# Short convolutions in PSUM and inverse roots by a power on GpSimd, in a hybrid attention and experts block

## The chip, the cores and the metric

The kernel runs on one core of a Trainium2 chip. A core has five engines with instruction queues of their own, each worked off in order: PE (matrix products), DVE (VectorE), ACT (ScalarE), POOL (GpSimd) and SP, which here only issues transfers. PE writes to PSUM, which has eight banks of 2 KB per partition; DVE and ACT read and write PSUM and SBUF, POOL only SBUF in this kernel. The metric is the device time of one execution in microseconds, as the median of three runs.

## The reference

One block over 256 latent tokens and 256 context tokens, 2048 features, all in float32. Cut to what bears on the change:

```python
h  = modulate(rms_norm(x, norm1_g), ...);  hc = modulate(rms_norm(ctx, norm1_g), ...)
glu, qkv, z, ab, br = split_in_proj(h @ w_in)          # and of hc
qkv = silu(dw_conv(qkv, short_w))                      # 5 taps along the tokens, per feature
q = q * rsqrt(sum(q*q, -1) + EPS) * 128 ** -0.5        # per head of 128 features
k = k * rsqrt(sum(k*k, -1) + EPS)
# per head, in both directions: gated delta rule in chunks, context first, then latents
o = rms_norm(o, dn_norm_g) * silu(z)
y = (sigmoid(br_a) * conv_module(glu) + sigmoid(br_b) * (o @ w_dn_out)) @ w_out
x = x + m2 * y
x = x + m5 * peer_experts(modulate(rms_norm(x, norm2_g), ...))
return rms_norm(x, final_g)
```

The convolution module has a layer norm of its own. So the inverse square root of a sum occurs in the norm of the inputs, of each head's q and k, of each head's output o, in the layer norm, in norm2 and in the final norm.

## The kernel before

**The weight stream.** All weights come from HBM as half tiles of 128 x 1024 float32. `prep` turns a half tile into two parts whose sum is exact: ACT casts `whi` (L201) and POOL or DVE subtracts `wlo` (L205); the table `SPLIT` says which, and for the heads ("a") it is always POOL. `mm3` (L209 to L212) makes one *product* of a block of 128 x 128 weights and 128 x 256 activations from three matmuls, `hi*hi + hi*lo + lo*hi`. `products` runs a weight tile's products into a PSUM bank `ps_p` per sequence, from a pool `psg` of three banks; the other five banks belong to the work between.

**The order.** All instructions of an engine stand in an order that is fixed when the kernel is built. Other work is written as generators, *chains*: a chain yields the number of products that are to be issued before its next step, by the table `GAP`. Several chains are under way at once, so steps of one head lie between steps of another on each engine's queue.

**The heads.** Sixteen heads follow each other. A head has 96 products (v 32, k 32 over both sequences, q 16 and z 16 over the latents alone), each projection followed by `short_conv` (z by a gate):

```python
for s in range(n):
    nc.scalar.copy(pd[:, s, 2:T + 2], ps[s])                                              # L593
    nc.scalar.activation(dst[:, s, :], ps[s], AF.Copy, scale=swh[:, blk, 2:3])            # L594
...
for i in (0, 1, 3, 4):
    nc.vector.scalar_tensor_tensor(dst, pd[:, :n, i:i + T], swh[:, blk, i:i + 1], dst, ALU.mult, ALU.add)  # L597
```

then a tanh on ACT (L600) and a last multiply on DVE (L602). `pd` is one of two padded buffers in SBUF, `dst` the result in SBUF. After q, the chain of a head goes through `prepare` (norms, keys and values by tokens, decays), `invert` (the triangular inverse, blocks doubling) and `scan` (four chunks, both directions). In `prepare`, sums of squares by ACT (L656, L666) get EPS on DVE (L667), their inverse root by `newton_steps` (L323, then three times L326, L328, L330, all on DVE, on 128 x 6 elements, with a gap of three products after each of the ten steps), and then, per direction, PE makes a decay's exponent (`ps_D`, L700 to L702), ACT its exponential (L704), DVE L709, L710 and L713, ACT L715, DVE L717 and POOL L718. The next direction's `ps_D` needs L713. In `scan`, the output's sums (L902) go through L904, `newton_steps` on 128 x 2 and a product with the factor of q (L907) to the scaling of `oacc` (L910), which PE transposes (L914).

**Elsewhere.** `inverse_rms` (L334) makes the same steps for the inputs, the layer norm, norm2 (L1269) and the final norm (L1522); the last two run with nothing beside them (`whole`).

After the heads come the first convolution gates, the branches' projections, `w_out` with norm2, the routing of the experts, their two dense passes, and the final norm.

Of the kernel before, what the change touches and what calls it, by code (L numbers as in the profile page):

```python
# [23 lines left out]
P = 128  # L24
D = 2048
# [21 lines left out]
GAP = dict(N=3, C0=3, C=3.5, P0=0.5, Pv=3, Pk=4, Pq=3, Pn=2.5, PG=3, PA=3.5, PD=2.5, Pat=2, Pkh=2, Pkl=1, L0=4,  # L47
           LX=4, LY=4.5, F0=7, FX=5, FY=5, FZ=2, IT=4.5, E=4, Z1=5, Z2=7, Sv=4, Sr=4, Sn=5, SS=6, So=3.5,
           Ss=1, Sf=3, Sa=2, Sg=5, So2=3,
           M=10, M0=2, DC=12, M1=16, MT=3, V=1.75, VA=2, VS=4.5, LN=4, NW=1, W=7, D=24, RT=5, RC=7, RB=11, H0=21, HP=12, G0=4)  # L50

# columns of the constants
# [5 lines left out]
# the parts of the modulation vectors in their order: vector, first column, columns  # L58
# [6 lines left out]
# columns of the parameters  # L65
# [35 lines left out]
# bytes per partition, buffers  # L101
# [27 lines left out]
def body(ctx: ExitStack, tc: tile.TileContext, a: dict, out: bass.AP):  # L129
# [14 lines left out]
    # A raw float32 half tile becomes two float32r parts whose sum is exact.  # L144
# [69 lines left out]
    # A chain is a generator: it yields how many products to issue before its next step.  # L214
# [22 lines left out]
    def products(keys, acts, sink, first):  # L237
        """The products of weight tiles, side by side, with each of the activations; what follows each."""
        pss = [[cur["psg"].tile([P, T], F32, name="ps_p", tag="g") for _ in acts] for _ in keys]
        halves = 1 if keys[0][0] == "peer_v" else 2  # L240
        for u in range(halves):
            ws = [parts.pop(0) for _ in keys]
            assert [w[0] for w in ws] == keys, (ws, keys)
            for c in range(8):
                for ps, (_, wh, wl) in zip(pss, ws):
                    for p_, (ah, al) in zip(ps, acts):
                        mm3(p_, wh[:, c, :], wl[:, c, :], ah[u][:, c, :], al[u][:, c, :],
                            u == 0 and c == 0, u == halves - 1 and c == 7)
# [28 lines left out]
    def mod_stream(mods, depth):  # L277
        """The weights' tiles for the parts mods of the vectors, loaded ahead of their products."""
# [14 lines left out]
    def mod_part(v, at, w, sc, alloc, psum_tile, following, gap):  # L293
        """Columns at ... at + w of vector v, one weight tile per step."""
# [12 lines left out]
        # column at + g * n + j * 128 + i at row 32 g  # L307
# [12 lines left out]
    def newton_steps(x, shape, gap, tag="sm"):  # L320
        """1 / sqrt(x) by Newton's steps from an estimate by the exponent."""
        y, t = cur["work"](shape, tag=tag, name="rsy"), cur["work"](shape, tag=tag, name="rst")
        nc.vector.tensor_scalar(y.bitcast(I32), x.bitcast(I32), -0.5, 1597463007.0, ALU.mult, ALU.add)  # L323
        yield gap
        for _ in range(3):
            nc.vector.tensor_tensor(t, y, y, ALU.mult)  # L326
            yield gap
            nc.vector.scalar_tensor_tensor(t, t, -0.5, x, ALU.mult, ALU.mult)  # L328
            yield gap
            nc.vector.scalar_tensor_tensor(y, t, 1.5, y, ALU.add, ALU.mult)  # L330
            yield gap
        return y

    def inverse_rms(acc, tag="d"):  # L334
        """1 / the root of the features' mean square, on every partition, from its sums per partition."""
# [8 lines left out]
        y = yield from newton_steps(ms, [P, n], GAP['NW'])  # L344
# [9 lines left out]
    if True:  # L354
# [63 lines left out]
        def scales(q):  # L418
            """For the feature chunks of part q."""
# [72 lines left out]
        # -30000 where a decay is of the future or of the token itself  # L492
# [23 lines left out]
        def decays():  # L516
# [8 lines left out]
            # column: chunk, direction, (a | b), head  # L525
# [22 lines left out]
            # log1p(e) = ln(u) + (e - (u - 1)) / u  # L548
# [15 lines left out]
            # sums of g from the chunk's first token, after the token, over the chunk  # L564
# [18 lines left out]
        def short_conv(ps, blk, dst):  # L583
            n = len(ps)
# [7 lines left out]
            for s in range(n):  # L592
                nc.scalar.copy(pd[:, s, 2:T + 2], ps[s])  # L593
                nc.scalar.activation(dst[:, s, :], ps[s], AF.Copy, scale=swh[:, blk, 2:3])  # L594
            yield GAP['C0']
            for i in (0, 1, 3, 4):
                nc.vector.scalar_tensor_tensor(dst, pd[:, :n, i:i + T], swh[:, blk, i:i + 1], dst, ALU.mult, ALU.add)  # L597
                yield GAP['C'] * n / 2
            th = pd[:, :n, 2:T + 2]
            nc.scalar.activation(th, dst, AF.Tanh)  # L600
            yield GAP['C'] * n / 2
            nc.vector.scalar_tensor_tensor(dst, th, 1.0, dst, ALU.add, ALU.mult)  # L602
# [29 lines left out]
        def prepare(x):  # L632
            """Norms, the keys and values by tokens, the products of keys, all decays."""
# [33 lines left out]
            nc.vector.tensor_scalar(ss, ss, EPS, None, ALU.add)  # L667
            yield GAP['Pq']
            rs = yield from newton_steps(ss, [P, 6], GAP['N'])
            rk = rs[:, 0:4]  # L670
            x.rq = work([P, 2], tag="sm")
            nc.vector.tensor_scalar(x.rq, rs[:, 4:6], float(P) ** -0.5, None, ALU.mult)
# [22 lines left out]
            # decay[j, i] = exp(sum of g over j < m <= i), then K = decay * (k_j . k_i)  # L695
# [26 lines left out]
        def invert(x):  # L722
            """The inverse of I + diag(beta) K^T per chunk and direction: blocks double in half
            precision, then two terms of the residual's series."""
# [50 lines left out]
            def product(lhs, rhs, name):  # L775
                """Per direction: a bank with the products of the four chunks."""
# [21 lines left out]
            # E = I - A T, then Z (I + E + E E)^T  # L798
# [26 lines left out]
        def scan(x):  # L825
            """The chunks in their order, both directions side by side; o, normed and gated."""
# [18 lines left out]
            for n in range(4):  # L845
# [36 lines left out]
                if n >= 2:  # L882
# [4 lines left out]
                    # each chunk of o is reached first by one direction, then by the other  # L887
# [38 lines left out]
        def glu_a(n, ps):  # L926
# [6 lines left out]
            nc.scalar.activation(half_a[n], ps[0], AF.Copy, scale=0.5)  # L933
            yield 1

        def glu_b(n, ps):
            ut = cur["work"]([P, T], tag="ut")
            nc.scalar.activation(ut, ps[0], AF.Tanh, scale=0.5)
# [9 lines left out]
        def taps(n, pr, cw, dst, gap):  # L948
            """The convolution over a raster row of chunk n of the features."""
# [14 lines left out]
        def convolution_a():  # L964
            """The first chunks, beside the last head's scan; they wait in DRAM for the others."""
# [16 lines left out]
        def follow(x, ps):  # L982
            """After a head's last projection."""
# [19 lines left out]
        first_jobs = [(("w_in", 64), (0, 1)), (("w_in", 48), (0, 1)), (("w_in", 32), (1,))]  # L1003
        free = [psg.tile([P, T], F32, name="ps_p", tag="g") for _ in range(3)] + [bank("ps_p")[:, :T] for _ in range(2)]
        pss = [[free.pop(0) for _ in seqs] for _, seqs in first_jobs]
# [594 lines left out]
```

## Time and profile before

| what | value |
|---|---|
| median of three runs | 3660.12 us (3659.87 to 3661.66) |
| span of the profiled execution | 3653.3 us |
| PE busy | 3394.9 us (93%) |
| DVE busy | 2342.5 us (64%) |
| POOL busy | 1802.3 us (49%) |
| ACT busy | 1501.4 us (41%) |

The profiled execution is known by its span alone, from its first instruction to its last; the runs' times also hold what lies around a span, so the median stands 6.8 us above it. Busy shares are means over stages: the heads lie at about 160 to 1380 us, the experts at about 2410 to 3640.

### The profile page before, as it was taken

How to read it: one execution, taken by the hardware profiler on the slowest of the kernel's cores; microseconds unless marked ns; L12 is line 12 of the kernel's file. 1: busy time of each engine (PE TensorE's matmuls, PEld its weight loads, DVE VectorE, ACT ScalarE, POOL GpSimd, SP SyncE). 2: the span in 40 equal slices, each digit the busy share in tenths (PEclk: the TensorE clock that was granted, in tenths of full speed). 3: DMA queues.
4: the chain of work that ended last, by engine and by line, in shares of the span. 5: the costliest groups of instructions: out<-in, count | busy, mean ns of one | idle time of the engine just before them, and what ended most of it. 6: DMA issues, size and time to landing. Idle time of an engine off the chain costs nothing.

```text
span 3653.3 us, 72163 instructions
## 1 busy us (share of the span) xinstructions
PE 3394.9 (93%) x29656; PEld 3237.3 (89%) x29656; DVE 2342.5 (64%) x4324; ACT 1501.4 (41%) x2723; POOL 1802.3 (49%) x895
## 2 busy tenths in 40 slices
PE   5788899999998889999998999999999999999998
PEld 3677777877888889999998999899999999999997
DVE  3468888888888869996766988842333333333446
ACT  2234344444444444444443444444444444444343
POOL 1343334434434568777546644354444455544554
PEclk9799999999999999999998999999999999999999
DMA  8633344443442245554554446465555555555554
GB/s 290 226 130 123 129 135 136 141 141 125 141 146 88 97 156 184 184 183 160 207 185 159 155 150 212 158 225 196 196 192 194 194 195 197 196 196 196 205 205 161
DMA packets 186170, 629.30 MB, mean 172 GB/s; under 512 B 19056, under 2 KB 23792, under 8 KB 182768
## 3 DMA queue, kind: packets, MB, share of 16 engines
q1 hardware_dynamic: 183104, 618.98, 50.1%
q10 hardware_dynamic: 2736, 5.71, 0.4%
q8 instruction: 233, 3.82, 0.4%
q14 instruction: 97, 0.79, 0.1%
HBM read 601.42 MB, written 23.20 MB: 171 GB/s over the span
## 4 chain that ended last, share of the span: by engine, by line
PE 51%; DVE 7%; issue 1%; POOL 1%; ACT 1%; DMA 1%; SPq 0%; DVEq 0%; POOLq 0%; ACTq 0%
PE ps_p L212 17%; PE ps_p L211 17%; PE ps_p L210 17%; PE ps_W L1414 1%; DVE oa L1391 1%; POOL wlo L205 1%; DVE wlo L205 1%; DVE ob L1392 1%; ACT whi L201 0%; DVE i L1309 0%; DVE sc L1310 0%; DVE i L1312 0%; DVE cand L1337 0%; DVE acc L1103 0%; DVE v L1311 0%
## 5 line engine op out<-in xcount | busy, mean ns | idle before, releaser
L205 POOL TENSOR_TENSOR wlo<-raw,whi 128x1024 fp32r<-128x1024 f32 x593 | 1453.4, 2452 | 1428.3 <-ACT whi L201 1373.4
L201 ACT CAST whi<-raw 128x1024 fp32r<-128x1024 f32 x896 | 938.3, 1049 | 1135.2 <-PE ps_p L211 786.0
L205 DVE TENSOR_TENSOR wlo<-raw,whi 128x1024 fp32r<-128x1024 f32 x303 | 424.7, 1402 | 846.9 <-ACT whi L201 843.4
L210 PE MATMUL ps_p<-hh,whi 128*128 128x256 f32 x2560 | 797.0, 311 | 2.7 <-ACT vT L594 1.4
L212 PE MATMUL ps_p<-hh,wlo 128*128 128x256 f32 x2560 | 732.6, 286 | 8.0 <-POOL wlo L205 7.8
L211 PE MATMUL ps_p<-hl,whi 128*128 128x256 f32 x2560 | 732.5, 286 | 0.0
L212 PE MATMUL ps_p<-h2h,wlo 128*128 128x256 f32 x2304 | 657.7, 285 | 12.2 <-DVE wlo L205 7.4
L210 PE MATMUL ps_p<-h2h,whi 128*128 128x256 f32 x2304 | 664.4, 288 | 3.3 <-ACT whi L201 1.6
L211 PE MATMUL ps_p<-h2l,whi 128*128 128x256 f32 x2304 | 657.1, 285 | 0.2 <-POOL h2l L1288 0.2
L212 PE MATMUL ps_p<-ph,wlo 128*128 128x256 f32 x2048 | 580.5, 283 | 2.1 <-POOL wlo L205 2.1
L211 PE MATMUL ps_p<-pl,whi 128*128 128x256 f32 x2048 | 579.7, 283 | 1.1 <-POOL pl L1463 1.0
L210 PE MATMUL ps_p<-ph,whi 128*128 128x256 f32 x2048 | 579.6, 283 | 0.3 <-ACT ph L1462 0.3
L210 PEld LDWEIGHTS ps_p<-hh,whi 128*128 128x128 f32 x2560 | 499.1, 195 | 61.2 <-issue 57.5
L212 PEld LDWEIGHTS ps_p<-hh,wlo 128*128 128x128 f32 x2560 | 497.8, 194 | 10.3 <-POOL wlo L205 10.3
L211 PEld LDWEIGHTS ps_p<-hl,whi 128*128 128x128 f32 x2560 | 500.0, 195 | 1.1
L212 PEld LDWEIGHTS ps_p<-h2h,wlo 128*128 128x128 f32 x2304 | 447.5, 194 | 13.4 <-DVE wlo L205 8.0
L210 PEld LDWEIGHTS ps_p<-h2h,whi 128*128 128x128 f32 x2304 | 447.8, 194 | 3.8 <-ACT h2h L1284 1.9
L211 PEld LDWEIGHTS ps_p<-h2l,whi 128*128 128x128 f32 x2304 | 447.8, 194 | 0.5 <-POOL h2l L1288 0.5
L212 PEld LDWEIGHTS ps_p<-ph,wlo 128*128 128x128 f32 x2048 | 393.1, 192 | 3.9 <-POOL wlo L205 3.9
L211 PEld LDWEIGHTS ps_p<-pl,whi 128*128 128x128 f32 x2048 | 393.1, 192 | 1.5 <-POOL pl L1463 1.5
L210 PEld LDWEIGHTS ps_p<-ph,whi 128*128 128x128 f32 x2048 | 393.1, 192 | 0.5 <-ACT ph L1462 0.5
L955 DVE SCALAR_TENSOR_TENSOR ps_cv<-up,cw,ps_cv 128x256 f32<-128x256 f32 x464 | 226.8, 489 | 14.5
(326 smaller groups left out, 5174.5 us busy)
## 6 DMA issues: line engine op xcount, KB each, us to landing
raw<-in_w_in_dram SPq DMA_DIRECT2D x256, 512.0 KB, 3.9
raw<-in_peer_u_dram SPq DMA_DIRECT2D x256, 512.0 KB, 4.2
raw<-in_peer_v_dram SPq DMA_DIRECT2D x256, 512.0 KB, 4.5
raw<-in_w_mod_dram SPq DMA_DIRECT2D x192, 512.0 KB, 3.8
raw<-in_w_dn_out_dram SPq DMA_DIRECT2D x32, 512.0 KB, 3.7
raw<-in_w_conv_out_dram SPq DMA_DIRECT2D x32, 512.0 KB, 4.2
raw<-in_w_out_dram SPq DMA_DIRECT2D x32, 512.0 KB, 3.9
raw<-in_w_q_dram SPq DMA_DIRECT2D x32, 512.0 KB, 3.6
```

The costliest lines, as they stand in the source:

```text
L201: nc.scalar.copy(hi, raw)
L205: eng.tensor_tensor(lo, raw, hi.bitcast(F32), ALU.subtract)
L210: nc.tensor.matmul(ps, wh, ah, start=start, stop=False)
L211: nc.tensor.matmul(ps, wh, al, start=False, stop=False)
L212: nc.tensor.matmul(ps, wl, ah, start=False, stop=stop)
L955: nc.vector.scalar_tensor_tensor(dst if i == CW - 1 else pr, up[n][:, :, i:i + GRID_W], cw[:, n, i:i + 1], pr, ALU.mult, ALU.add)
L1391: nc.vector.tensor_scalar(oa, iota, slots[:, 0, t:t + 1], slots[:, 2, t:t + 1], ALU.is_equal, ALU.mult)
L1392: nc.vector.tensor_scalar(ob, iota, slots[:, 1, t:t + 1], None, ALU.is_equal)
L1414: nc.tensor.matmul(pw[:, j, :], ob, oa, start=True, stop=True)
```

## The change

Four edits. (1) `products` gives both sequences one bank, `[P, len(acts), T]`, in place of one each; the first matmul of the bank alone starts it. The first head's products use three banks of `psg` and no longer two others besides. (2) `short_conv` copies and scales both sequences by one ACT instruction each, the scaled product stays in PSUM, and the taps and the tanh work on it there; the last multiply writes to SBUF. (3) `newton_steps` goes; `inverse_root` is one `tensor_tensor` with `pow` and a tile of -0.5 on GpSimd. In `prepare` and `scan` the additions ahead of it move to GpSimd as well, L667's and L904's; the product L907 becomes L910's second scalar, and constant factors move into a parameter (`Q_GN`), scaled once. (4) Gaps: ten gaps of three products after Newton steps become one of ten (`N`), `Pq`, `Ss` and `Sf` go, `So` is 12 in place of 3.5, `NW` 2 in place of 1. A head's chain has gaps of 222.25 products in all, 270.75 before.

```diff
-        pss = [[cur["psg"].tile([P, T], F32, name="ps_p", tag="g") for _ in acts] for _ in keys]
+        pss = [cur["psg"].tile([P, len(acts), T], F32, name="ps_p", tag="g") for _ in keys]
...
-                    for p_, (ah, al) in zip(ps, acts):
-                        mm3(p_, wh[:, c, :], wl[:, c, :], ah[u][:, c, :], al[u][:, c, :],
-                            u == 0 and c == 0, u == halves - 1 and c == 7)
+                    for s, (ah, al) in enumerate(acts):
+                        mm3(ps[:, s, :], wh[:, c, :], wl[:, c, :], ah[u][:, c, :], al[u][:, c, :],
+                            u == c == s == 0, u == halves - 1 and c == 7 and s == len(acts) - 1)
...
+    minus_half = cst.tile([P, 8], F32, name="minus_half")
+    nc.gpsimd.memset(minus_half, -0.5)
...
+    def inverse_root(y, x):
+        nc.gpsimd.tensor_tensor(y, x, minus_half[:, :x.shape[1]], ALU.pow)
...
-        y = yield from newton_steps(ms, [P, n], GAP['NW'])
+        y = work([P, n], tag="sm")
+        inverse_root(y, ms)
+        yield GAP['NW']
...
-            for s in range(n):
-                nc.scalar.copy(pd[:, s, 2:T + 2], ps[s])
-                nc.scalar.activation(dst[:, s, :], ps[s], AF.Copy, scale=swh[:, blk, 2:3])
+            nc.scalar.copy(pd[:, :n, 2:T + 2], ps)
+            nc.scalar.activation(ps, ps, AF.Copy, scale=swh[:, blk, 2:3])
             yield GAP['C0']
             for i in (0, 1, 3, 4):
-                nc.vector.scalar_tensor_tensor(dst, pd[:, :n, i:i + T], swh[:, blk, i:i + 1], dst, ALU.mult, ALU.add)
+                nc.vector.scalar_tensor_tensor(ps, pd[:, :n, i:i + T], swh[:, blk, i:i + 1], ps, ALU.mult, ALU.add)
                 yield GAP['C'] * n / 2
             th = pd[:, :n, 2:T + 2]
-            nc.scalar.activation(th, dst, AF.Tanh)
+            nc.scalar.activation(th, ps, AF.Tanh)
             yield GAP['C'] * n / 2
-            nc.vector.scalar_tensor_tensor(dst, th, 1.0, dst, ALU.add, ALU.mult)
+            nc.vector.scalar_tensor_tensor(dst, th, 1.0, ps, ALU.add, ALU.mult)
...
-            nc.vector.tensor_scalar(ss, ss, EPS, None, ALU.add)
-            yield GAP['Pq']
-            rs = yield from newton_steps(ss, [P, 6], GAP['N'])
-            rk = rs[:, 0:4]
-            x.rq = work([P, 2], tag="sm")
-            nc.vector.tensor_scalar(x.rq, rs[:, 4:6], float(P) ** -0.5, None, ALU.mult)
+            rs = work([P, 6], tag="sm")
+            nc.gpsimd.tensor_scalar(ss, ss, EPS, None, ALU.add)
+            inverse_root(rs, ss)
+            yield GAP['N']
+            rk, x.rq = rs[:, 0:4], rs[:, 4:6]
...
+            fo = work([P, 2], tag="sm")
+            nc.gpsimd.tensor_scalar(so, so, float(P) ** 2 * EPS, None, ALU.add)
+            inverse_root(fo, so)
             yield GAP['So']
-            nc.vector.tensor_scalar(so, so, 1.0 / P, EPS, ALU.mult, ALU.add)
-            yield GAP['Ss']
-            fo = yield from newton_steps(so, [P, 2], GAP['N'])
-            nc.vector.tensor_tensor(fo, fo, x.rq, ALU.mult)
-            yield GAP['Sf']
             for c in range(2):
-                nc.vector.tensor_scalar(oacc[:, c, :], oacc[:, c, :], fo[:, c:c + 1], None, ALU.mult)
+                nc.vector.tensor_scalar(oacc[:, c, :], oacc[:, c, :], fo[:, c:c + 1], x.rq[:, c:c + 1], ALU.mult,
+                                        ALU.mult)
```

## Rows read from the trace of the kernel before

**Rows 1.** Windows: length; busy PE, PEld, DVE, ACT, POOL; clock, DMA share, GB/s.

```profile
160.00:1380.00 1220.00, 1093.00 (x10280) 978.12 (x10279) 989.24 (x1937) 513.34 (x1231) 528.28 (x275) 0.97 0.39 129
2410.00:3640.00 1230.00, 1221.91 (x10155) 1219.07 (x10153) 449.00 (x544) 507.98 (x605) 632.80 (x281) 1.00 0.59 198
```

**Rows 2.** PE's waits, 160 to 1380 us (total, times, longest), four of 24.

```profile
PE ps_D L700 <- DVE De L713: 25.2, 13, 2.4
PE ps_Z L781 <- DVE E L811: 17.0, 17, 1.2
PE ps_oT L914 <- DVE oacc L910: 11.2, 5, 6.4
...
PE ps_D L700 <- DVE rst L326: 1.7, 1, 1.7
```

**Rows 3.** DVE over 160 to 1380 us: L597, L602, tile rst.

```profile
160.00:1380.00 1220.00, 199.08 (x192) 0.97 0.39 129
...
160.00:1380.00 1220.00, 38.72 (x48) 0.97 0.39 129
...
160.00:1380.00 1220.00, 138.55 (x288) 0.97 0.39 129
```

**Rows 4.** Groups by form, 160 to 1380 us: L667, L904, L907.

```profile
L667 DVE TENSOR_SCALAR sm<-sm 128x6 f32<-128x6 f32 x16 | 27.4, 1714 | 22.7 <-ACT jp L666 22.7
...
L904 DVE TENSOR_SCALAR sm<-sm 128x2 f32<-128x2 f32 x16 | 13.5, 844 | 0.0
...
L907 DVE TENSOR_TENSOR rsy<-rsy,sm 128x2 f32<-128x2 f32 x16 | 15.9, 993 | 0.0
```

**Rows 5.** Source lines: shortest, median, longest ns, first and last start.

```profile
L597 DVE SCALAR_TENSOR_TENSOR vT<-pad,pf,vT x64: 735/745/2928, 169.2 to 1153.6; 128x512 f32<-128x512 f32 x64
...
L597 DVE SCALAR_TENSOR_TENSOR q<-pad,pf,q x64: 469/484/2597, 184.2 to 1195.9; 128x256 f32<-128x256 f32 x64
...
L602 DVE SCALAR_TENSOR_TENSOR vT<-pad,vT x16: 673/677/2457, 182.0 to 1157.1; 128x512 f32<-128x512 f32 x16
...
L326 DVE TENSOR_TENSOR rst<-rsy x96: 139/160/2350, 201.0 to 1335.0; 128x6 f32<-128x6 f32 x48, 128x2 f32<-128x2 f32 x48
```

**Rows 6.** Timeline of one stall in head 7; last brackets: idle time and releaser.

```profile
693.85 2.39 POOL L205 TENSOR_TENSOR wlo<-raw,whi 128x1024 fp32r<-128x1024 f32 x1
693.93 2.33 DVE L330 SCALAR_TENSOR_TENSOR rsy<-rst,rsy 128x2 f32<-128x2 f32 x1
...
696.18 0.67 DVE L713 TENSOR_TENSOR De<-Gs,ps_D 128x512 f32<-128x512 f32 x1
...
697.00 0.47 PE L700 MATMUL ps_D<-Lg,st 128*128 128x512 f32 x1 [1.69 <-DVE De L713]
```

**Rows 7.** POOL's smallest instruction, and its splits, by source line.

```profile
L1588 POOL MEMSET const-float32-0.0<- x1: 99/99/99, 0.2 to 0.2; 128x1 f32 x1
...
L205 POOL TENSOR_TENSOR wlo<-raw,whi x162: 2344/2388/2934, 168.0 to 1378.9; 128x1024 fp32r<-128x1024 f32 x162
```

**Rows 8.** Groups by form: one operation from PSUM and from SBUF.

```profile
L1253 DVE SCALAR_TENSOR_TENSOR x<-ps_p,modL,x 128x256 f32<-128x256 f32 x16 | 7.7, 484 | 9.5 <-PE ps_p L212 9.5
...
L1476 DVE SCALAR_TENSOR_TENSOR x<-yT,modL,x 128x256 f32<-128x256 f32 x16 | 7.8, 485 | 4.3 <-DMA x<-x2d 3.7
```

**Rows 9.** Timeline of DVE at norm2: around the ten Newton steps.

```profile
1936.81 0.16 DVE L343 TENSOR_SCALAR sm<-ps_tok 128x2 f32<-128x2 f32 x1 [1.11 <-PE ps_tok L340]
...
1938.97 0.48 DVE L347 TENSOR_SCALAR dg<-cc,rsy 128x128 f32<-128x128 f32 x2
```

**Rows 10.** Source lines that stay, DVE, 160 to 1380 us.

```profile
L710 DVE COPY_PREDICATED at<-diag,As x32: 444/666/1847, 219.4 to 1237.3; 128x256 f32<-128x256 uint16 x32
...
L717 DVE TENSOR_TENSOR kk<-kk,c x32: 424/426/2153, 224.3 to 1240.9; 128x512 f16<-128x512 f16 x32
...
L910 DVE TENSOR_SCALAR oacc<-oacc,rsy x32: 274/279/298, 374.5 to 1343.5; 128x128 f32<-128x128 f32 x32
```

**Rows 11.** Window of line L210 on PE, as head 1's products begin.

```profile
170.00:175.00 5.00, 3.85 (x14) 2.66 (x14) 1.00 0.44 133
```

More of the change, by code (lines that the diff above doesn't have):

```diff
@@ L45 @@
 Z_AT = (1, 4)
[L47 to L50, printed above, removed]
+GAP = dict(N=10, C0=3, C=3.5, P0=0.5, Pv=3, Pk=4, Pn=2.5, PG=3, PA=3.5, PD=2.5, Pat=2, Pkh=2, Pkl=1, L0=4,
+           LX=4, LY=4.5, F0=7, FX=5, FY=5, FZ=2, IT=4.5, E=4, Z1=5, Z2=7, Sv=4, Sr=4, Sn=5, SS=6, So=12,
+           Sa=2, Sg=5, So2=3,
+           M=10, M0=2, DC=12, M1=16, MT=3, V=1.75, VA=2, VS=4.5, LN=4, NW=2, W=7, D=24, RT=5, RC=7, RB=11, H0=21, HP=12, G0=4)
 C_ID, C_ONE, C_IO, C_TF, C_TB, C_SF, C_SB, C_BD, C_IC = 0, 128, 256, 384, 512, 640, 768, 896, 1024
@@ L318, in mod_part @@
         yield GAP['MT']
[L320 to L332, printed above, removed]
+    def inverse_root(y, x):
+        nc.gpsimd.tensor_tensor(y, x, minus_half[:, :x.shape[1]], ALU.pow)
     def inverse_rms(acc, tag="d"):
@@ L371, in body @@
         nc.vector.tensor_scalar(pf[:, Q_SW:Q_SW + 240], pf[:, Q_SW:Q_SW + 240], 0.5, None, ALU.mult)
+        nc.vector.tensor_scalar(pf[:, Q_GN:Q_GN + 1], pf[:, Q_GN:Q_GN + 1], float(P) ** 0.5, None, ALU.mult)
         sc = cst.tile([P, NCH, 32], F32, name="sc")
@@ L583, in short_conv @@
         def short_conv(ps, blk, dst):
-            n = len(ps)
+            n = ps.shape[1]
             i_pad = n_pad[0] % 2
@@ L626, in in_z @@
             zt = work([P, T], tag="zt")
-            nc.scalar.activation(x.zh, ps[0], AF.Copy, scale=0.5)
+            nc.scalar.activation(x.zh, ps[:, 0, :], AF.Copy, scale=0.5)
             nc.scalar.activation(zt, x.zh, AF.Tanh)
@@ L932, in glu_a @@
             half_a[n] = cur["work"]([P, T], tag="ua")
-            nc.scalar.activation(half_a[n], ps[0], AF.Copy, scale=0.5)
+            nc.scalar.activation(half_a[n], ps[:, 0, :], AF.Copy, scale=0.5)
             yield 1
@@ L937, in glu_b @@
             ut = cur["work"]([P, T], tag="ut")
-            nc.scalar.activation(ut, ps[0], AF.Tanh, scale=0.5)
+            nc.scalar.activation(ut, ps[:, 0, :], AF.Tanh, scale=0.5)
             yield 1
@@ L1003, in body @@
         first_jobs = [(("w_in", 64), (0, 1)), (("w_in", 48), (0, 1)), (("w_in", 32), (1,))]
-        free = [psg.tile([P, T], F32, name="ps_p", tag="g") for _ in range(3)] + [bank("ps_p")[:, :T] for _ in range(2)]
-        pss = [[free.pop(0) for _ in seqs] for _, seqs in first_jobs]
+        pss = [psg.tile([P, len(seqs), T], F32, name="ps_p", tag="g") for _, seqs in first_jobs]
         ps_ab = [bank("ps_ab0", "s"), bank("ps_ab1", "p")]
@@ L1022, in first_products @@
                     _, wh, wl = ws[j]
-                    for p_, s in zip(pss[j], first_jobs[j][1]):
-                        mm3(p_, wh[:, e, :], wl[:, e, :], hh[s][u][:, e, :], hl[s][u][:, e, :], c == 0, c == NCH - 1)
+                    seqs = first_jobs[j][1]
+                    for k, s in enumerate(seqs):
+                        mm3(pss[j][:, k, :], wh[:, e, :], wl[:, e, :], hh[s][u][:, e, :], hl[s][u][:, e, :],
+                            c == k == 0, c == NCH - 1 and k == len(seqs) - 1)
                         tick()
@@ L1195, in br_dn @@
             gates.append(gt)
-            nc.scalar.activation(gt, ps[0], AF.Tanh, scale=0.5)
+            nc.scalar.activation(gt, ps[:, 0, :], AF.Tanh, scale=0.5)
             yield 1
         def dn_out(n, ps):
-            gated(gates[n], ps[0], at(yd, n))
+            gated(gates[n], ps[:, 0, :], at(yd, n))
             dn_done.append(n)
@@ L1209, in br_conv @@
         def br_conv(n, ps):
-            nc.scalar.activation(at(gts, n), ps[0], AF.Tanh, scale=0.5)
+            nc.scalar.activation(at(gts, n), ps[:, 0, :], AF.Tanh, scale=0.5)
             yield 1
@@ L1218, in conv_out @@
             mg = work([P, T], tag="mg")
-            gated(at(gts, n), ps[0], mg)
+            gated(at(gts, n), ps[:, 0, :], mg)
             yield 1
@@ L1252, in w_out @@
             xo = at(x2, n)
-            nc.vector.scalar_tensor_tensor(xo, ps[0], modL[:, 2, n:n + 1], xo, ALU.mult, ALU.add)
+            nc.vector.scalar_tensor_tensor(xo, ps[:, 0, :], modL[:, 2, n:n + 1], xo, ALU.mult, ALU.add)
             yield 1
@@ L1319, in w_q @@
             q_ = work([P, T], tag="qf")
-            nc.scalar.copy(q_, ps[0])
+            nc.scalar.copy(q_, ps[:, 0, :])
             yield 8
@@ L1436, in u_sink @@
         def u_sink(g, j, ps):
-            nc.scalar.activation(G[g][:, j, :], ps[0], AF.Gelu_apprx_tanh)
+            nc.scalar.activation(G[g][:, j, :], ps[:, 0, :], AF.Gelu_apprx_tanh)
             yield 1
@@ L1469, in v_sink @@
             if g == 0:
-                nc.scalar.copy(yo, ps[0])
+                nc.scalar.copy(yo, ps[:, 0, :])
             else:
-                nc.vector.tensor_tensor(yo, ps[0], yo, ALU.add)
+                nc.vector.tensor_tensor(yo, ps[:, 0, :], yo, ALU.add)
             if g == NGRP - 1:
```

## The prediction

> **What bounds the kernel now.** I read the windows by stage first. The reader should compare two stages of nearly equal length. From 2410 to 3640 us PE is busy 1221.9 of 1230 us at full granted clock: nothing in the change can win there. From 160 to 1380 us, the heads, PE is busy 1093.0 of 1220 us at a clock of 0.97, and DVE is busy 989.2 us, 81% [rows 1]. So the heads stage holds 127 us in which PE idles, and 0.03 of 1220 = 37 us lost to the lower clock. These are the stocks that the change can draw on; most of its edits lie here.
>
> Next I read PE's waits in that stage, to see who ends them. The ten kinds of wait on DVE that average 0.9 us or more sum to 95.2 us, from L713's 25.2 us in 13 waits down to 1.7 us in one wait for a Newton step; the tail of the last heads is among them, with 11.2 us for L910 in 5 waits, the longest 6.4 [rows 2]. No POOL or ACT row is of that size.
>
> Then I asked why DVE is late although 19% of it is free. The sums by line and the spread of single durations answer it. A Newton step on 128x6 or 128x2 elements has a median of 0.160 us and a longest of 2.35 [rows 5]; a short-convolution tap on v has a median of 0.745 and a longest of 2.93 [rows 5]. Both read two operands in SBUF. The timeline of one stall shows what stretches them: POOL's split begins at 693.85 and takes 2.39, a Newton step on two columns begins at 693.93 and ends as the split does, 2.33 later; L713 behind it starts at 696.18, and PE, which needs L713's result, waits 1.69 [rows 6]. POOL runs 162 such splits in the stage [rows 7] and is busy 43% of it [rows 1]. DVE's queue is in order, so a tiny instruction of one head blocks another head's decay.
>
> **The change part by part: DVE.** Newton removed: the 288 steps on tile rst and rsy cost 138.6 us [rows 3], the additions and the product around them (L667, L904, L907) 27.4 + 13.5 + 15.9 [rows 4]: 195 us in all. Unblocked, 336 instructions at 0.16 would be 54; so 141 of the 195 us is blocked time. L907's product goes into L910 as a second scalar, costed at nothing: L910 is 0.28 us [rows 10] and a scalar per partition adds no element.
>
> Short convolution: the same 240 instructions remain, with one of two inputs now in PSUM. They cost 199.1 + 38.7 = 237.8 us [rows 3]. At unblocked medians (128 on 512 columns by 0.745, 64 on q by 0.484, 32 last ones by 0.677, 16 by an estimated 0.44 in q's proportion) they cost 95.4 + 31.0 + 21.7 + 7.0 = 155 [rows 5], 83 less. Bounds: 0, if an operand in PSUM doesn't lift the blocking, to 83. I take 83, because with one SBUF operand left the instruction resembles L910, which has one and never exceeded 0.298 in 32 runs beside the same splits [rows 10].
>
> That a PSUM operand costs the same per instruction is read from 128x256 with it, 484 ns, and without, 485 [rows 8]. [...]
>
> DVE so falls by 195 + 83 = 278 us, from 989 to about 711 of 1220, 58%; 224 of the 278 was blocked time.
>
> **From DVE's time to PE's.** Only waits count. Not all of the 95.2 us goes: L710 (median 0.666, longest 1.847) and L717 (longest 2.153) still read two SBUF operands [rows 10] and sit on the decays' path just ahead of PE's wait. Bounds are 48 (half) and 95 (all); I take three quarters, **-71**.
>
> The clock: PE that waits less is granted more. Of 37 us I take a quarter, **-9** (bounds 0 and -37).
>
> **What is added.** POOL gets 16 x 2 pairs of an addition and a power, on 128x6 and 128x2. No row shows a power on POOL. Bounds: 0.10 us, POOL's smallest instruction, and 2.39, a split of 1024 columns [rows 7]. I take 1.0, with 0.2 for the addition: 32 x 1.2 = 38 us, POOL 43 to 46%, hidden behind PE, as splits are made ahead of their products. The chain waits for it in a gap of ten products (12 in the scan). Fifteen heads of 96 products lie between the first tap on v at 169.2 and the last at 1153.6 [rows 5], 0.68 us a product, so the gap is 6.8 us.
>
> The powers issue in POOL's order, with the splits queued behind them and the sums on ACT ahead of them. Once a power ends, a queued split starts at once, and the DVE instruction that needs the power's result starts beside it. If that instruction loses half a split: 32 x 0.43 x 1.2 = 16.5 us of DVE, of which I let half reach PE, **+8** (bounds 0 and 16.5). The row for it is L910, whose 32 runs show no loss so far [rows 10]. [...]
>
> Products: both sequences share a bank, held until the last multiply of the convolution, about 20 gaps after the product's end, in place of ACT's two copies. With three banks a bank comes round after the next two products, 48 weight products for v. That covers it in steady state. Not for head 1's v: head 0's last multiply on v begins at 182.0 [rows 5], and PE already runs products at full rate from 170 to 175 [rows 11], so the one that needs this bank is late by 0 to 8 us: **+4**, once.
>
> ACT: a copy and a scale over 512 columns replace two each of 256: a few tenths less per product, ACT being 42% busy [rows 1]: nothing.
>
> The gaps: a head's chain is 270.75 products long before and 222.25 after. It removes no work, and overlap with the next heads remains; nothing by itself. If the in-order queues meet otherwise, that is in the bounds above.
>
> Norm2 and the final norm are serial: from L343 to L347 1938.97 - 1936.81 = 2.16 us before [rows 9], of which ten steps at 0.195 are 1.95. A power of 1.0 and a hop of 0.2 between engines give -0.75 each, **-1.5** (bounds -3 and +1.3). The start's and layer norm's same chains run beside weight transfers and products: nothing, and -1 each if that cover is gone.
>
> Sum: -71 - 9 + 8 + 4 - 1.5 = **-69.5** on the profiled span of 3653.3, 3583.8. The median of the runs lies 6.8 us above that span (3660.1), so 3590.6: I forecast **3590**.
>
> **The rivals.** *Waits return elsewhere.* PE's waits are partly latency, not queueing: E L811 delays it 17 times by 1.0 us on average [rows 2], as a dependent step would. If each removed stall merely uncovers the next wait (on POOL's ordered queue, on L710), half of the 95 goes and the clock gives nothing: -48 + 12 + the rest, near 3622; with the queue at its upper bound, 3630. Range 3620 to 3650. For: many kinds of small waits. Against: the timeline, where the stall ends exactly with the split.
>
> *The power is long (slower).* One mechanism: the power's time on POOL against the gap of 6.8 us. Take off the addition 0.2, ACT's two sums ahead of it 0.6 (0.28 each, L910's time on the same 128x128 [rows 10]) and half a split 1.2, and 4.8 us is left; beyond it the chain's next DVE instruction stands at the head of DVE's queue and PE stalls as now. The gain of 70 is eaten when 32 x (t - 4.8) = 70, at t = 7.0 us. At 8 us: 32 x 3.2 = 102 less 70 is +32, near 3692. For: no row of it, and a power isn't one elementary step. Against: POOL handles 131,072 elements in 2.39 us [rows 7], and the power has at most 768.
>
> *It doesn't do what it says.* If one operand in PSUM leaves the blocking as it is, 83 of DVE's 278 us stays: 50 us of waits go in place of 71, 3611, inside my range. No change at all needs the bank's hold to give back the gain: DVE so late that each head waits 4 us for a bank, 16 x 4 = 64, near 3654.
>
> *More than I say.* All 95.2 and half the clock: -95 - 18 + 10 = -103, 3557 and below.
>
> **How the numbers follow.** Forecast case (3555 to 3620) 0.62; more, below 3555, 0.06; waits return (3620 to 3650) 0.18; no change 0.05; slower 0.09. Within 0.2%, 7.3 us, this kernel's measurement can't tell from no change. The range 3550 to 3645 leaves out the slower and unchanged cases and the ends of two others, about 2 in 10. Faster 0.86, same 0.05, slower 0.09.
>
> **What would show it.** DVE 690 to 740 us in the heads stage, L597's longest near its median, PE's waits for L713 under 10 us, the clock 0.98 or more; a power row under 2.4 us on POOL. I am wrong if taps from PSUM still reach 2 us, if PE waits for ps_p's bank behind L602 in every head, or if new PE waits end on POOL's power.

## The result, and the profile after

The changed kernel took 3610.89 us as the median of four runs (3604.04 to 3613.96), the kernel before 3659.99 beside it. The ratio on record is 0.9876, with a 95% interval of 0.9857 to 0.9895; the two medians alone divide to 0.9866. That is 45 us less by the ratio and 49 by the medians, where 70 were forecast. Faster, then, clear of the noise though by less than 2%, and inside the range; but the sum behind it was wrong in two terms that offset each other, as the experiments below show.

One thing of the part ahead of the prediction has to be set right. A time lies about 2 us above the span of the same execution (3613.96 and 3612.2 us for the profiled one after the change), and not 6.8: that number compared two executions. The forecast isn't touched, as it comes to the median before less 69.5.

The windows by stage after the change, with the columns of [rows 1]; the first is the heads stage, which now ends some 30 us earlier, the second the experts:

```profile
160.00:1350.00 1190.00, 1081.01 (x10303) 970.20 (x10302) 799.07 (x1566) 501.63 (x1175) 562.99 (x344) 0.98 0.42 135
2360.00:3600.00 1240.00, 1231.87 (x10229) 1229.28 (x10227) 452.49 (x559) 512.54 (x617) 636.60 (x283) 1.00 0.60 197
```

The experts stage is as it was. A better comparison takes the stretch from the first tap on a head's v to the last head's short convolutions, which holds nearly the same work in both. First the kernel before, then the one after, same columns:

```profile
169.00:1195.00 1026.00, 923.07 (x8791) 813.22 (x8789) 847.71 (x1673) 430.65 (x1061) 409.55 (x212) 0.97 0.40 130
```

```profile
162.00:1155.00 993.00, 906.87 (x8832) 801.85 (x8831) 673.19 (x1356) 414.62 (x1003) 428.36 (x267) 0.98 0.42 135
```

It shrank by 33 us (1026 to 993). Another 7 of the 41 us between the two spans (3653.3 and 3612.2) lie ahead of it: the first tap starts at 162.2 in place of 169.2, and at 160.1 to 165.2 in the experiments. The prediction put nothing there, and no run separates what did it. In the stretch DVE fell by 174.5 us, where 278 were costed for the whole stage. The short convolutions and the power came out nearly as costed, first as source lines (shortest, median, longest ns), then as groups of POOL (sum in us, mean ns):

```profile
L592 DVE SCALAR_TENSOR_TENSOR ps_p<-pad,pf,ps_p x192: 475/744/757, 162.2 to 1155.1; 128x512 f32<-128x512 f32 x128, 128x256 f32<-128x256 f32 x64
...
L903 DVE TENSOR_SCALAR oacc<-oacc,sm x32: 334/342/3190, 326.4 to 1279.5; 128x128 f32<-128x128 f32 x32
```

```profile
L324 POOL TENSOR_TENSOR sm<-sm,minus_half 128x6 f32<-128x6 f32 x16 | 21.6, 1352 | 1.3
...
L324 POOL TENSOR_TENSOR sm<-sm,minus_half 128x2 f32<-128x2 f32 x19 | 13.5, 713 | 5.7 <-DVE sm L335 4.4
```

The taps, with one operand in PSUM, never exceed 0.757 us; before, they reached 2.93 [rows 5]. They still meet POOL: 61 of the 192 begin while it has over 0.3 us of an operation to run, and none is held, where before 55 of 59 such taps were, for 0.67 to 2.18 us beyond their medians. The operand in PSUM shows no price of its own: over 512 columns the median is 0.747 us, as 0.745 before, and the last multiply, with one operand in PSUM and its result in SBUF, takes 0.680 on average, where its median was 0.677 [rows 5]. The power takes 0.71 us on two columns and 1.35 on six.

The lost DVE time is in the groups (sum and mean) of two instructions that had not been blocked before:

```profile
L722 DVE TENSOR_TENSOR Tf<-Tc,c 128x1024 f16<-128x1024 f16 x15 | 34.2, 2283 | 0.5
...
L625 DVE SCALAR_TENSOR_TENSOR z<-zt,z 128x256 f32<-128x256 f32 x14 | 27.8, 1983 | 12.4 <-ACT zt L623 12.4
```

Before the change these means were 0.69 and 0.41 us:

```profile
L728 DVE TENSOR_TENSOR Tf<-Tc,c 128x1024 f16<-128x1024 f16 x14 | 9.7, 692 | 0.5
...
L630 DVE SCALAR_TENSOR_TENSOR z<-zt,z 128x256 f32<-128x256 f32 x14 | 5.7, 410 | 0.0
```

Both read two operands in SBUF, and a split now lies over them in nearly every head: all 16 gates take 1.97 us or more, and 13 of 16 Tf 2.50 or more. PE's waits in the heads stage show where that ends:

```profile
PE ps_X L744 <- DVE kk L711: 27.8, 14, 3.8
PE ps_X L775 <- DVE Tf L722: 16.4, 12, 1.7
PE ps_p L210 <- DVE vT L597: 9.1, 1, 9.1
PE ps_D L694 <- DVE De L707: 8.9, 8, 2.3
...
PE ps_oT L908 <- DVE oacc L903: 4.7, 2, 2.4
```

The wait for L713 (now L707) fell from 25.2 to 8.9 and that for the scan's tail from 11.2 to 4.7 [rows 2]. New at the top stands a wait of 27.8 us in 14 for the masked keys (`kk`). Before the change it was this one:

```profile
PE ps_X L750 <- DVE kk L717: 5.8, 4, 2.6
```

Last, the timeline of one of the 14:

```profile
1184.77 0.98 DVE L704 COPY_PREDICATED at<-diag,As 128x256 f32<-128x256 uint16 x1
...
1185.40 2.54 POOL L205 TENSOR_TENSOR wlo<-raw,whi 128x1024 fp32r<-128x1024 f32 x1
...
1185.77 2.46 DVE L625 SCALAR_TENSOR_TENSOR z<-zt,z 128x256 f32<-128x256 f32 x1
...
1188.15 0.68 DVE L707 TENSOR_TENSOR De<-Gs,ps_D 128x512 f32<-128x512 f32 x1
...
1189.51 0.42 DVE L711 TENSOR_TENSOR kk<-kk,c 128x512 f16<-128x512 f16 x1 [0.68 <-ACT kk L709]
...
1189.99 0.27 PE L744 MATMUL ps_X<-c,kk 128*128 128x32 f16 x4 [2.56 <-DVE kk L711]
```

It is the old pattern [rows 6] with another victim: a split begins at 1185.40, another head's z gate at 1185.77 takes 2.46 us, to 0.29 us past that split's end, the decay steps behind it follow, and PE waits 2.56 us.

The serial norm2, on DVE and POOL: L335 to L341 is now 0.96 us, against 2.16 for the same pair [rows 9].

```profile
1892.69 0.16 DVE L335 TENSOR_SCALAR sm<-ps_tok 128x2 f32<-128x2 f32 x1 [1.11 <-PE ps_tok L332]
1892.92 0.69 POOL L324 TENSOR_TENSOR sm<-sm,minus_half 128x2 f32<-128x2 f32 x1 [1.63 <-DVE sm L335]
1893.65 0.48 DVE L341 TENSOR_SCALAR dg<-cc,sm 128x128 f32<-128x128 f32 x2 [0.81 <-POOL sm L324]
```

### The profile page after: what moved, and what is told of

It is laid out like the page before. It is cut to its first block, busy times and chain, and to the rows that moved or that the text cites. A ratio compares the mean times of both kernels' runs of the same rounds, so it can differ in the third digit from the quotient of the medians.

```text
span 3612.2 us, 71826 instructions
## 1 busy us (share of the span) xinstructions
PE 3378.1 (94%) x29656; PEld 3225.7 (89%) x29656; DVE 2139.3 (59%) x3901; ACT 1483.2 (41%) x2659; POOL 1828.2 (51%) x964
## 4 chain that ended last, share of the span: by engine, by line
PE 51%; DVE 7%; issue 2%; POOL 2%; ACT 1%; DMA 1%; SPq 0%; ACTq 0%; POOLq 0%; DVEq 0%
PE ps_p L212 16%; PE ps_p L211 16%; PE ps_p L210 16%; PE ps_W L1409 1%; DVE oa L1386 1%; POOL wlo L205 1%; DVE wlo L205 1%; DVE ob L1387 1%; ACT whi L201 1%; DVE cand L1332 0%; DVE i L1304 0%; DVE sc L1305 0%; DVE i L1307 0%; DVE v L1306 0%; POOL pl L1458 0%
## 5 line engine op out<-in xcount | busy, mean ns | idle before, releaser
L210 PE MATMUL ps_p<-hh,whi 128*128 128x256 f32 x2560 | 792.3, 310 | 11.0 <-DVE vT L597 9.1
L210 PE MATMUL ps_p<-h2h,whi 128*128 128x256 f32 x2304 | 665.1, 289 | 2.7 <-ACT h2h L1279 1.6
L210 PE MATMUL ps_p<-ph,whi 128*128 128x256 f32 x2048 | 579.5, 283 | 0.0
L210 PEld LDWEIGHTS ps_p<-hh,whi 128*128 128x128 f32 x2560 | 495.7, 194 | 69.5 <-issue 67.1
L210 PEld LDWEIGHTS ps_p<-h2h,whi 128*128 128x128 f32 x2304 | 448.3, 195 | 3.2 <-ACT h2h L1279 1.9
L210 PEld LDWEIGHTS ps_p<-ph,whi 128*128 128x128 f32 x2048 | 393.1, 192 | 0.0
```

The source lines that it names most:

```text
L210: nc.tensor.matmul(ps, wh, ah, start=start, stop=False)
```

## The experiments

All times are medians; each ratio is to the kernel before on the same chip at the same time (3650.9 to 3653.2 us there). On that scale the change itself, 0.9876, is about 3607 us.

**Taps back in SBUF.** In place of PSUM the SBUF result is the accumulator, for the tanh and the last multiply too (not shown); the shared bank and the power stay.

```diff
-            nc.scalar.activation(ps, ps, AF.Copy, scale=swh[:, blk, 2:3])
+            nc.scalar.activation(dst, ps, AF.Copy, scale=swh[:, blk, 2:3])
...
-                nc.vector.scalar_tensor_tensor(ps, pd[:, :n, i:i + T], swh[:, blk, i:i + 1], ps, ALU.mult, ALU.add)
+                nc.vector.scalar_tensor_tensor(dst, pd[:, :n, i:i + T], swh[:, blk, i:i + 1], dst, ALU.mult, ALU.add)
```

> The changed kernel, but the short convolution's taps, tanh and last multiply work on their SBUF result again (one bank per product and the power on GpSimd stay). Theory (DVE instructions with two SBUF operands are blocked by POOL's splits, and that blocking sets PE's waits): taps reach 2.3 us or more again, DVE in the heads rises by 50 to 90 us, and of the 49 us gained the convolution's part, 83 of 278, comes back: about 3626 us (3618 to 3635). Rival (the shorter gaps alone made the gain): within 7 us of 3611.

3677.32 us, ratio 1.0068 (1.0055 to 1.0082): slower than before the change. The taps are blocked again (first line, a source line), and PE's waits for the decays and the scan's state grow (second and third):

```profile
L592 DVE SCALAR_TENSOR_TENSOR vT<-pad,pf,vT x64: 734/1300/2857, 161.4 to 1178.4; 128x512 f32<-128x512 f32 x64
```

```profile
PE ps_D L694 <- DVE De L707: 42.8, 15, 3.4
...
PE ps_o L879 <- DVE S L872: 16.0, 14, 1.7
```

So the power and the shorter gaps without the PSUM taps lose 25 us. The direction was the theory's; the size, 70 us over the change, was more than four times its 15.

**Newton kept.** The kernel before with the shared bank and the PSUM taps alone, old gaps (the diff's hunks on `products`, the first products and `short_conv`).

> The kernel before with the convolution's part alone: one bank per product, taps in PSUM; Newton steps on VectorE and the old gaps stay. Theory (blocked DVE): taps never above 0.8 us, Newton steps still up to 2.35 us, 83 of 278 of the gain: about 3645 us (3635 to 3652). Rival (gaps, or the power alone): 3655 to 3665. Third (convolution alone made it): 3611 to 3620.

3600.08 us, 0.9855 (0.9841 to 0.9868). This part alone makes what the whole change makes. The theory asked for 15 us and got 53, more than any of the three expectations allowed.

**Old gaps.** The changed kernel with as many products in a chain as before.

```diff
-GAP = dict(N=10, ... So=12, ... NW=2, ...)
+GAP = dict(N=33, ... So=37.5, ... NW=10, ...)
```

> The changed kernel with the old total gaps of a chain: 33 products after the power in the preparation, 37.5 in the scan, 10 in the layer norm. Theory (blocked DVE): the gain stays, 3605 to 3622 us. Rival (the shorter chain made the gain): 3645 to 3660 us. Were the waits of the chain on POOL's power part of the time, it would be below 3605.

3517.69 us, 0.9625 (0.9612 to 0.9638). With its gaps undone the change gains 136 us, so shortening the gaps had cost about 90. Neither theory had this. Only the expectation's last case, that the chain waits for POOL's power, lies below 3605, and the late start further down rules it out. The window of its head stretch (columns of [rows 1]), then PE's waits, then DVE groups:

```profile
160.70:1066.70 906.00, 883.06 (x8775) 787.00 (x8774) 674.51 (x1337) 421.51 (x998) 426.88 (x268) 0.99 0.46 147
```

```profile
PE ps_p L210 <- DVE vT L597: 9.1, 1, 9.1
...
PE ps_X L744 <- DVE kk L711: 4.3, 3, 1.8
...
PE ps_D L694 <- DVE De L707: 1.9, 6, 1.0
```

```profile
L794 DVE TENSOR_TENSOR IT<-c,Tf 128x1024 f16<-128x1024 f16 x14 | 30.9, 2208 | 0.0
L711 DVE TENSOR_TENSOR kk<-kk,c 128x512 f16<-128x512 f16 x30 | 25.9, 865 | 14.3 <-ACT kk L709 14.3
L625 DVE SCALAR_TENSOR_TENSOR z<-zt,z 128x256 f32<-128x256 f32 x14 | 25.9, 1847 | 1.5 <-ACT zt L623 0.3
```

Here the theory falls, as it stood. DVE is busy 674.5 us in this stretch and 673.2 in the changed kernel, with as much blocking (the z gate at 1.85 us a time, the identity less the product, L794, at 2.21). Yet the stretch is 87 us shorter and PE's wait for the masked keys is 4.3 us. So what counts isn't DVE's blocked sum. It may be whether blocked instructions stand in front of one that PE is waiting for; the next kernels test this.

**The second theory: place.** Program order on DVE, from a listing of the kernels' instructions, changed kernel first, then with 33 products in the preparation's gap:

```text
936 L592 SCALAR_TENSOR_TENSOR ps_p<-pad_506,pf,ps_p 128x512
...
939 L592 SCALAR_TENSOR_TENSOR ps_p<-pad_506,pf,ps_p 128x512
940 L703 TENSOR_TENSOR at<-As,ps_D 128x256
941 L704 COPY_PREDICATED at<-diag,As 128x256
942 L592 SCALAR_TENSOR_TENSOR ps_p<-pad_506,pf,ps_p 128x512
943 L707 TENSOR_TENSOR De<-Gs,ps_D 128x512
944 L711 TENSOR_TENSOR kk<-kk,c_481 128x512
945 L592 SCALAR_TENSOR_TENSOR ps_p<-pad_506,pf,ps_p 128x512
946 L703 TENSOR_TENSOR at<-As,ps_D 128x256
947 L704 COPY_PREDICATED at<-diag,As 128x256
948 L625 SCALAR_TENSOR_TENSOR z<-zt,z 128x256
949 L707 TENSOR_TENSOR De<-Gs,ps_D 128x512
950 L711 TENSOR_TENSOR kk<-kk,c_481 128x512
```

```text
923 L625 SCALAR_TENSOR_TENSOR z<-zt,z 128x256
...
926 L597 SCALAR_TENSOR_TENSOR vT<-pad_506,ps_p 128x512
...
935 L703 TENSOR_TENSOR at<-As,ps_D 128x256
936 L704 COPY_PREDICATED at<-diag,As 128x256
937 L707 TENSOR_TENSOR De<-Gs,ps_D 128x512
938 L711 TENSOR_TENSOR kk<-kk,c_481 128x512
939 L703 TENSOR_TENSOR at<-As,ps_D 128x256
940 L704 COPY_PREDICATED at<-diag,As 128x256
941 L707 TENSOR_TENSOR De<-Gs,ps_D 128x512
942 L711 TENSOR_TENSOR kk<-kk,c_481 128x512
```

With the short gap two taps on v stand just ahead of the eight decay steps of a head (L703, L704, L707, L711, twice), and two more and the z gate among them, in 14 of 16 heads by the trace. With the longer gap no tap and no z gate is among them in 15 of 16, and the z gate comes ahead. The gap shifts everything from the decays on against the convolutions, which are tied to the products. The rival: each product of gap is worth something by itself, as more room. Four kernels tell them apart.

**33 products in the preparation alone** (`N=10` to `N=33`).

> The changed kernel with the old total gap in the preparation alone (33 products after the power on q and k; the scan keeps 12). Place theory (the preparation's gap decides which instructions of other heads stand in VectorE's queue around the decay steps): nearly the whole gain of the old gaps, 3515 to 3540 us, and PE's wait of 27.8 us for the masked keys below 10. Length theory (each product of gap is worth the same, 23 of 48.5): about 3565 us.

3520.74 us, 0.9646 (0.9632 to 0.966): nearly the whole gain, with an interval that overlaps that of the old gaps. PE's wait for the masked keys:

```profile
PE ps_X L744 <- DVE kk L711: 5.1, 3, 2.4
```

**37.5 products in the scan alone** (`So=12` to `So=37.5`).

> The changed kernel with the old total gap in the scan alone (37.5 products after the power on the output; the preparation keeps 10). Place theory: little, 3590 to 3612 us, the wait for the masked keys stays above 20 us, since the scan's tail holds only a scaling and a multiply on VectorE. Length theory (25.5 of 48.5 products): about 3560 us.

3602.02 us, 0.9867 (0.9852 to 0.9882): no difference from the change, so length by itself is worth nothing there. One clause of the expectation failed: the wait for the masked keys fell to 5.8 us. The tail of another head's scan now falls just ahead of it on PE, and PE waits there instead, 17.8 us in 23 waits, about half of them ended by DVE and half by ACT:

```profile
PE ps_oT L908 <- ACT vn L859: 9.1, 12, 1.1
...
PE ps_oT L908 <- DVE oacc L903: 8.7, 11, 2.5
```

**22 products in the preparation** (`N=22`, `So=37.5`).

> The changed kernel with 22 products in the preparation's gap, between 10 and 33, and the old 37.5 in the scan. Length theory (93 us over 48.5 products, evenly): 11 products short, about 3539 us. Place theory: no even scale; anything from 3515 to 3620 us, and away from 3539 by more than 10 us, as other instructions meet.

3567.61 us, 0.9784 (0.9768 to 0.9799), 29 us off the even scale; the place theory had left nearly everything open here. PE's waits are others:

```profile
PE ps_D L694 <- DVE De L707: 17.2, 15, 1.9
PE ps_vn L857 <- DVE r L848: 12.9, 13, 1.6
PE ps_X L753 <- DVE Tc L747: 10.0, 13, 1.1
```

**Newton steps with short gaps** (the second experiment with `N=0.7`, `Sf=0.5`: a chain as long as the change's).

> The kernel with taps in PSUM and Newton steps kept (3600 us with the old gaps), its gaps shortened so that a chain is as long as in the change: 0.7 after each Newton step, 10 and 12 in all. If the shorter gaps cost by themselves, whatever makes the inverse root: 3650 to 3710 us. If they cost only together with the power on GpSimd: 3590 to 3615 us.

3651.07 us, 1.0000 (0.9991 to 1.0009): the shorter gaps cost 51 us with Newton steps too. The wait for the masked keys is there again, as large as in the change (27.5 against 27.8), and one for the scan's tail:

```profile
PE ps_oT L914 <- DVE oacc L910: 29.7, 14, 6.9
PE ps_X L750 <- DVE kk L717: 27.5, 14, 3.8
```

Over the stretch from the first tap to the last short convolution's last tap, these kernels stand as follows; PE's waits are the sum of all rows of its waits in the stretch:

| kernel | stretch, us | PE's waits, us | DVE busy, us |
|---|---|---|---|
| before | 1026 | 101.9 | 847.7 |
| Newton kept | 974 | 68.4 | 780.4 |
| Newton, short gaps | 1027 | 104.7 | 737.0 |
| taps in SBUF | 1058 | 126.9 | 758.5 |
| the change | 993 | 85.4 | 673.2 |
| scan's gap 37.5 | 994 | 82.1 | 676.3 |
| preparation's gap 22 | 966 | 65.5 | 692.0 |
| preparation's gap 33 | 914 | 26.7 | 672.8 |
| old gaps | 906 | 22.6 | 674.5 |

The stretch goes with PE's waits and not with DVE's time: Newton steps with short gaps keep DVE 43 us less busy than with the old ones and take 53 us longer.

**A later start of the preparation** (`P0=0.5` to `P0=23.5`, the gap after the power stays 10).

> The changed kernel, its gaps after the powers as changed, but the preparation begins 23 products later (gap P0 23.5 in place of 0.5), so that everything from the decays on stands at the same products as with 33 after the power. Place theory: 3515 to 3540 us, as with the longer gap after the power. Rival (the gap of ten products is too short for the sums on ACT and the power on GpSimd): within 15 us of 3608.

3523.91 us, 0.9650 (0.9635 to 0.9665), as with the longer gap after the power; PE waits 4.6 us for the masked keys. So the gap of ten isn't too short for the power; the rival of a long power is out, and the shift alone does it.

**The z gate in PSUM**, at the short gap and at the long:

```diff
-            nc.scalar.activation(x.zh, ps[:, 0, :], AF.Copy, scale=0.5)
-            nc.scalar.activation(zt, x.zh, AF.Tanh)
+            half = ps[:, 0, :]
+            nc.scalar.activation(half, half, AF.Copy, scale=0.5)
+            nc.scalar.activation(zt, half, AF.Tanh)
             yield 2
-            nc.vector.scalar_tensor_tensor(x.zh, zt, 1.0, x.zh, ALU.add, ALU.mult)
+            nc.vector.scalar_tensor_tensor(x.zh, zt, 1.0, half, ALU.add, ALU.mult)
```

> The changed kernel with the head's z gate too working on its PSUM bank, so its multiply on VectorE (mean 1.98 us after the change, 0.41 before it) has one SBUF operand left. Theory (the blocking that the change took away has in part moved to other instructions with two SBUF operands, at the same place in each head): the multiply falls to 0.4 to 0.5 us, PE's wait of 27.8 us in 14 times for the masked keys (ps_X for kk) falls below 10 us, and the time to 3590 to 3603 us. Rival (that wait is a plain dependence of PE on DVE and ACT in a row): the wait stays over 20 us and the time within 7 us of 3611.

> 33 products after the power in the preparation, and the z gate on its PSUM bank. Place theory: with the decay steps away from the z gate the blocking of that multiply hardly reaches PE any more, so little: 3508 to 3522 us against 3521. If the z gate's blocking costs wherever it stands, as at the short gap (24 us): about 3497 us.

At the short gap 3587.03 us, 0.9808 (0.9794 to 0.9823), some 25 less than the change by the ratios and 3 below the range expected; the gate is at 0.42 us, and PE's wait behind it halves from 27.8, though it doesn't fall below 10:

```profile
L626 DVE SCALAR_TENSOR_TENSOR z<-zt,ps_p 128x256 f32<-128x256 f32 x14 | 5.9, 420 | 11.8 <-ACT zt L624 11.8
```

```profile
PE ps_X L745 <- DVE kk L712: 14.1, 15, 2.2
```

At the long gap 3522.19 us, 0.9650 (0.9634 to 0.9666): nothing, though the gate falls from 1.34 us on average (the line is that of 33 products alone) to 0.41:

```profile
L625 DVE SCALAR_TENSOR_TENSOR z<-zt,z 128x256 f32<-128x256 f32 x16 | 21.5, 1342 | 1.9 <-ACT zt L623 1.8
```

The same unblocked instruction is worth 25 us where the decay steps stand behind it and nothing where they don't. This is the plainest evidence for place.

**The first head's v in SBUF**, on top of the long gap and the z gate in PSUM, so that its bank comes free early (the taps, the tanh and the last multiply use `acc` too, not shown):

```diff
+            acc = dst if early else ps
-            nc.scalar.activation(ps, ps, AF.Copy, scale=swh[:, blk, 2:3])
+            nc.scalar.activation(acc, ps, AF.Copy, scale=swh[:, blk, 2:3])
```

> The same, and the first head's convolution of v alone accumulates in SBUF, so its bank comes free after ACT's two operations. If the wait of 9.1 us for that bank is a loss of its own: 9 us less than the run with the z gate alone, and no wait for L598's vT. If other work of the start (the decays' sums, 3.0 us before the change) stands right behind it: 0 to 6 us less.

3520.15 us, 0.9641 (0.9625 to 0.9657): 2 us less than without it (4 by the spans of the profiled executions), which the intervals don't tell from nothing. The wait of 9.1 us is gone, and the decays' sums take 2.5 us of it back:

```profile
PE ps_cum L563 <- DVE gg L554: 2.5, 1, 2.5
```

**One scalar per partition in the scan's scaling**, the product on GpSimd behind the power:

```diff
+            nc.gpsimd.tensor_tensor(fo, fo, x.rq, ALU.mult)
...
-                nc.vector.tensor_scalar(oacc[:, c, :], oacc[:, c, :], fo[:, c:c + 1], x.rq[:, c:c + 1], ALU.mult,
-                                        ALU.mult)
+                nc.vector.tensor_scalar(oacc[:, c, :], oacc[:, c, :], fo[:, c:c + 1], None, ALU.mult)
```

> The changed kernel with the product of the two factors on GpSimd, behind the power, and one scalar per partition in the scaling of the head's output (as before the change, when its longest was 0.298 us in 32). After the change its longest is 3.19 us in 32. If the place (right behind the power, where a split starts) causes that: still one or more over 1 us. If the second scalar does: none over 0.4 us. Time within 7 us of 3608 either way.

3614.02 us, 0.9898 (0.9881 to 0.9914), the change's interval overlapped. The source line still reaches 3.42 us:

```profile
L904 DVE TENSOR_SCALAR oacc<-oacc,sm x32: 273/278/3422, 326.2 to 1279.2; 128x128 f32<-128x128 f32 x32
```

So it isn't the second scalar.

The best kernel here is the change with its old gaps: 3518 us, and 3521 with the preparation's gap alone.

## Why the prediction was right, and where it was wrong

*What bounds the kernel*: right. The stock was PE's idle time and clock in the heads, 164 us. The best version gained 136, some 120 of them in the head stretch (1026 to 906).

*Unblocking*: right for each instruction costed (taps 0.745, the power's 0.71 and 1.35 around the 1.0 taken, norm2 -1.2 us where -0.75 was taken). The argument for the taps was unsound all the same. That one SBUF operand left is safe was read from L910's 32 runs "beside the same splits" [rows 10], but none of these began beside a POOL operation with over 0.3 us to run. The additions L667 and L904, with one SBUF input as well, were held in 15 and 7 of 16 runs (1.71 and 0.84 us on average [rows 4]), and after the change so was the scaling of L910 itself, now L903. The taps came free with an operand in PSUM; that they would was in part luck.

The step from DVE's time to PE's was mis-sized: -71 and -9 for the clock stood in the sum. In the change itself PE's waits in the stretch fell by 16 us only (101.9 to 85.4), and its busy time by as much. At unchanged gaps taps and power gave 53 us and another 84 (0.9855 to 0.9625): 136 in all. The power without the taps wasn't run at the old gaps, so the split holds in this order. I had capped the waits at the 95 us read by name and taken a quarter of the clock; in the stretch PE's busy sum fell from 923 to 883 us as the clock rose from 0.97 to 0.99, and with the waits nearly all gone, PE's idle time there fell from 103 to 23.

*"It removes no work, and overlap with the next heads remains; nothing by itself"*: this is the step that failed. The shorter gaps cost 90 us with the power and 51 with Newton steps. I had looked at a chain's length only and not at what it shifts: everything behind the gap moves against the convolutions by 23 products, and on DVE's ordered queue that decided who stood before whom (two taps and the z gate among the decay steps in 14 of 16 heads, or in one at most). The two errors, 136 against 80 and 90 against 0, cancelled to 45 or 49 against 70: that the time fell inside the range was luck.

*DVE to 711 us*: it came to 799 in the stage, where 690 to 740 was the sign. In the stretch 46 us of blocking went over to the z gate (14 times 1.57) and to Tf (15 times 1.59). Besides, a sum by lines counts instructions that overlap twice: the stage's durations add to 1098 us before and 871 after, where DVE is busy 989 and 799, so of a fall of 227 only 190 is DVE's. The rival "waits return elsewhere" named the right kind of loss, and the kernel came out at its edge, but for a reason it didn't have: the gaps, not latency.

*L910 behind the power* (L903 after): 32 of them take 17.2 us of DVE after the change and 7.6 before, some 2 of it for the second scalar (0.342 against 0.279 unblocked); of the 16.5 us bounded about half came. Six scalings begin beside a POOL operation, and all six are held until it or POOL's next one ends: they take 1.07 to 3.19 us, and end 0.08 to 0.15 us after it. What makes them wait no run shows. Of the 8 us that I let reach PE 4.7 came: PE's two waits for this line both stand behind held scalings, one of them here:

```profile
1230.55 2.34 POOL L205 TENSOR_TENSOR wlo<-raw,whi 128x1024 fp32r<-128x1024 f32 x1 [0.46 <-ACT whi L201]
1230.57 2.66 DVE L903 TENSOR_SCALAR oacc<-oacc,sm 128x128 f32<-128x128 f32 x2
...
1233.03 0.58 PE L908 MATMUL ps_oT<-cc,oacc 128*128 128x128 f32 x2 [2.34 <-DVE oacc L903]
```

*Head 1's bank*: the wait came, 9.1 us where I took 4, but taking it away gave 2 us, within the noise; the decays' sums take 2.5 of it back.

*Slower by a long power*: out, by the power's own rows and by the late start.

What stays open: what makes the rest of the 90 us. The z gate's share is measured (25 us). That the four taps cost as well is argued from the order, not shown, and they can't be all of it: PE's wait for Tf, 16.4 us at the short gap, is gone with 33 products, and Tf isn't among the decay steps. There the split lies over L794 instead, for which PE hardly waits. Nor does everything among the decay steps cost: with the old gaps the two scalings and the multiply of a scan stand there in 13 of 16 heads, in the fastest kernel. The runs with 22 products show that other meetings cost other sums, so 33 need not be the best gap either.

## What to carry to other kernels

A blocked instruction on VectorE's ordered queue cost here what stood behind it: freeing the z gate's multiply was worth 25 us with the decay steps behind it and nothing without them. So read, for each engine, who follows whom in a period of the schedule; its busy sum told little here (673.2 and 674.5 us of DVE in stretches 87 us apart). When an edit comes with a retuned gap or offset, run the edit with the old offset too: here the edit was worth 136 us and the new offset took 90 of it back. And where taps with two operands in SBUF waited for GpSimd, up to 2.93 us, one of them in PSUM ended it here (0.757 at most) at no price per instruction (medians of 0.747 and 0.745 us); one SBUF operand without another in PSUM was no safeguard, as the scaling's 3.19 us shows.

## What the runs showed of the hardware

That a scaling on VectorE with a single SBUF input can be held by GpSimd, six of 32 after the change, I had not expected from its 32 unblocked runs before [rows 10]; as said, none of them began beside a POOL operation with over 0.3 us to run. So what freed the taps isn't just that one SBUF operand was left. The scaling is held by a memset too, which reads nothing. In the changed kernel, by the timeline, a pair of scalings from 1278.14 takes 3.26 us; its second one begins at 1279.51 and ends 0.15 us after the memset that POOL began at 1279.44:

```profile
1278.14 3.26 DVE L903 TENSOR_SCALAR oacc<-oacc,sm 128x128 f32<-128x128 f32 x2
...
1279.44 1.81 POOL L923 MEMSET up<- 128x2048 f32 x1
```

The run with one scalar shows it again: the second scaling lasts from 1279.24 to 1281.12, the memset from 1279.17 to 1280.97.
